# A two-block network on one core: the attention block takes tokens before their norm factor, and the factor is applied to the projections

## The chip, the cores and the metric

One core of a Trainium2 chip runs the whole program. The metric is the device time of one execution in microseconds; lower is better. In the profile the engines are PE (matrix multiply; PEld its weight loads), DVE (vector), ACT (scalar), POOL (GpSimd) and SP (which issues the DMAs). Each runs its own instructions strictly in program order and waits on semaphores for the others.

## The reference, cut to what matters

256 tokens of width 1024, float32. The first block has two layers: a mixer and a dense feed-forward, then a mixer and a mixture of eight experts (two a token); it ends in an RMS norm. The second block is an attention block over 16 learned meta tokens and the 256 tokens:

```python
x = first_block(...)                       # ends: rms_norm(x, norm_final)
h = concatenate([pad, meta, x])
xn = rms_norm_2(h, norm_gain)
proj = xn @ w_in                           # sb_q sb_k sb_v sw_q sw_k sw_v sb_z sw_z g_sb g_sw
o_sb = stick_breaking_attention(sb_q, sb_k, sb_v)       # 8 heads of 64
o_sw = sliding_window_sink_attention(rope(sw_q), rope(sw_k), sw_v, sinks)   # 16 heads on 2
y_sb, y_sw = (o_sb * silu(sb_z)) @ w_sb, (o_sw * silu(sw_z)) @ w_sw
h = h + (sigmoid(g_sb) * y_sb + sigmoid(g_sw) * y_sw) @ w_out
out = rms_norm_2(h, final_norm_gain)
```

So a token is normed twice in a row on its way into `w_in`: x·r1·gf (end of block one), then ·r2·g2. Per token both norms are one number r = r1·r2 and one row of weights gf·g2, and r can be applied before the projection or to its results.

## The kernel before, in words

Every matrix product is made of three float32r products: each operand is split into a high part (`whi`, `hi`) and the rest (`wlo`, `lo`), and PE adds hi·hi, hi·lo and lo·hi (`mm3`, L341 to L343). A weight unit is 128x1024 values. `Stream` (L158) brings raw tiles of two units by DMA, and `split` turns each unit into `whi` on ACT (L226) and `wlo` on DVE or POOL (L228), as the `plan` says per tile. `next` hands units to PE and splits some units ahead; every engine does its part at that place of its own order.

Experts: 88 chunks of 256 hidden columns. Chunk c does the two halves of its gate and up products, transposes chunk c-1's activation (`aH` on ACT, `aL` on DVE) and multiplies it by the down weights (`y`). `overflow` at chunk 85 is a branch round a large body that runs only when an expert has more than 128 tokens. After the last chunk `combine` adds the eighth expert's result to the tokens.

Entry to attention (`c_norms`, `phase_c`): per half of the tokens, sum of squares of x, x·gf, sum of squares of that, both factors, x·gf·r2·g2, PE transposes to `hT` (hi copied by ACT, lo subtracted by DVE), with 20 idle products (`warm`) on PE. Then the values `pv`, the keys and queries of the stick-breaking heads (8 projections `pj`), and a loop over those heads.

That loop is threaded with 38 further projections of 128 columns, the fills F0 to F37, in the order k, v, q0, z0, q1, z1, ... q7, z7, z8 to z11, g0 to g15. A fill is 24 matmuls into one of two PSUM buffers (tag `mm`), so fill n+2 waits until fill n's result has been read. `F` issues a fill and then the second steps of earlier ones: for q (and k) ACT copies the result (L1713), POOL turns it by the rope in six instructions (L1719 to L1721), and one fill later DVE and POOL place it as `qs` (L1469, L1470). For z and g ACT copies the result at once (L1476).

Iteration i of the loop (i = 0 to 7): `sb2(i)` (PE `sp`, DVE `lb` L1690, ACT exponent), F for q_i, `sb1(i+2)` (PE `zs`; three logs on ACT, `s`, `lb`, `sL` on DVE), F for z_i, and at odd i `sb3` (PE `av`). Then eight turns j of the sliding attention with two fills each: `sw1b(j)` scales the probabilities `pr` on DVE (L1783 to L1790), `sw1(j+1)` makes scores `sc` and their softmax (DVE reductions L1762, L1763, ACT exponents L1776), `sw2(j)` transposes (`pT`, L1800), `sw2b(j)` multiplies by the values (`ov`, L1818). `sw1(0)` runs in iteration 7 after that iteration's first fill.

Of the kernel before, what the change touches and what calls it, by code (L numbers as in the profile page):

```python
# [36 lines left out]
C_ID, C_BD, C_TRI, C_IOTA, C_LT, C_G2 = 0, 128, 256, 384, 512, 576  # L37
# [120 lines left out]
class Stream:  # L158
# [99 lines left out]
class K:  # L258
# [92 lines left out]
    def plan(self):  # L351
# [23 lines left out]
        if self.stop != "B":  # L375
            p += [(I["w_c"][i], i < 2 or 16 <= i < 24) for i in range(35)]
        return p

    def run(self):
        nc, tc = self.nc, self.tc  # L380
        with ExitStack() as es:
# [5 lines left out]
            ring = en(tc.tile_pool(name="ring", bufs=1))  # L387
            self.x = self.cs.tile([P, 2, D], F32, tag="x", name="x")
            self.con = self.cs.tile([P, C_N], F32, tag="con", name="con")
# [18 lines left out]
            if self.stop != "CX":  # L408
                with tc.tile_pool(name="ringx", bufs=1) as ringx, ExitStack() as es2:
                    self.W.add(ringx, self.RAW[1], self.HL[1])  # L410
                    self.ph = es2.enter_context(tc.tile_pool(name="ph", bufs=1))
# [9 lines left out]
            else:  # L421
                self.c_loads()
                self.c_g2()
                self.c_meta()
                self.c_meta2()
                self.c_rows()
                with tc.tile_pool(name="pj", bufs=1) as pj:
                    self.c_norms([lambda ns: 0] * 2, pj.tile([P, 512], F32, tag="junk", name="junk"))
# [8 lines left out]
    def phase_a(self):  # L437
# [4 lines left out]
        nc.sync.dma_start(self.con[:, P:], I["consts"][:, P:])  # L442
# [338 lines left out]
    def gln1b(self, g):  # L781
        self.nc.tensor.matmul(g[0][:, S:], self.con[:, C_BD:C_BD + P], g[1], start=True, stop=True)
# [141 lines left out]
    def phase_b(self):  # L924
# [8 lines left out]
        for c in range(N + 1):  # L933
# [18 lines left out]
            if 0 < c <= N:  # L952
# [3 lines left out]
                w = self.W.next(2, ahead=4 if c < N - 1 else 2)  # L956
# [7 lines left out]
            if c < N and e % 2 == 1 and e + 1 < NE:  # L964
# [4 lines left out]
                elif i == 9:  # L969
                    self.onehot_t(e // 2 + 1)  # L970
            if c == N - 3:
# [12 lines left out]
        if self.stop != "B":  # L984
            self.c_norms(comb, self.t2("junk"))
# [187 lines left out]
    def overflow(self):  # L1173

        nc, tc, pb = self.nc, self.tc, self.pb
        n = nc.values_load(self.cnt[0:1, 0:1], min_val=0, max_val=S)
# [5 lines left out]
        w = self.ph.tile([P, 2048], F32, tag="hx2", name="ov_w")  # L1182
# [4 lines left out]
        with tc.If(n > P):  # L1187
# [75 lines left out]
    def c_meta2(self):  # L1263
# [4 lines left out]
        self.metaT = self.cs.tile([P, KD, NM], F32, tag="metaT", name="metaT")  # L1268
        nc.scalar.activation(self.metaT, p[:, 0:P].rearrange("p (k t) -> p k t", k=KD), AF.Copy)
# [6 lines left out]
    def c_norms(self, before, junk):  # L1276

        nc, sm = self.nc, self.sm
        V, A = nc.vector, nc.scalar
        xn = [sm.tile([P, D], F32, tag="xn", name="xn", bufs=2) for _ in range(2)]  # L1280
        ss, v, r = [[sm.tile([P, n], F32, tag=t, name=t, bufs=2) for _ in range(2)]
                    for t, n in (("ss4", 4), ("nv", 3), ("nr", 2))]
        half = [slice(h * 512, h * 512 + 512) for h in range(2)]
        self.cx = [(xn[b], r[b]) for b in range(2)]

        def add(b, n):
            before[b](ns=(n,))
            x = self.x[:, b, half[n]]
            A.activation(junk, x, AF.Square, scale=1.0 / 32, accum_out=ss[b][:, n:n + 1])

        def gain(b, n, eng=V):
            y = xn[b][:, half[n]]
            eng.tensor_mul(y, self.x[:, b, half[n]], self.gf[:, half[n]])

        def power(b, n):
            y = xn[b][:, half[n]]
            A.activation(junk, y, AF.Square, scale=1.0 / 32, accum_out=ss[b][:, 2 + n:3 + n])

        def root(b):
            s, t = ss[b], v[b]  # L1300
            V.tensor_scalar(t[:, 0:1], s[:, 0:1], s[:, 1:2], EPS, op0=ALU.add, op1=ALU.add)
            V.scalar_tensor_tensor(t[:, 2:3], t[:, 0:1], EPS, s[:, 2:3], op0=ALU.mult, op1=ALU.add)
            V.tensor_add(t[:, 1:2], t[:, 2:3], s[:, 3:4])
            nc.gpsimd.tensor_tensor(r[b], t[:, 0:2], self.mhalf[:, 0:1].to_broadcast([P, 2]), op=ALU.pow)

        def scale(b, n):
            y = xn[b][:, half[n]]
            V.scalar_tensor_tensor(y, y, r[b][:, 1:2], self.g2[:, half[n]], op0=ALU.mult, op1=ALU.mult)
        for n in range(2):
            add(0, n)  # L1310
            gain(0, n)
            power(0, n)
        add(1, 0)
        root(0)
        self.W.release()
        self.W.ahead(3)
        add(1, 1)
        self.warm(20)
        scale(0, 0)
        gain(1, 0)  # L1320
        scale(0, 1)

        def rest():
            gain(1, 1)
            power(1, 0)
            power(1, 1)
            root(1)
            scale(1, 0)
            scale(1, 1)
        self.c_rest = rest  # L1330

    def phase_c(self):
        nc, pc, W, I = self.nc, self.pc, self.W, self.I
        V, A, mm = nc.vector, nc.scalar, nc.tensor.matmul
        hT = [pc.tile([P, KD, NK], F32R, tag="hT%d" % i, name="hT") for i in range(2)]
        self.split_small(self.metaT, *[t[:, :, 0:NM] for t in hT])
        W.ahead(4)
        self.transpose_split(self.cx[0][0], hT[0], hT[1], NM)
        self.c_rest()
# [3 lines left out]
        self.rep16 = self.t1("rep16")[0:48, 0:P]  # L1343
        for r in (slice(0, 32), slice(32, 48)):
            nc.vector.tensor_copy(self.rep16[r].rearrange("p (h c) -> p h c", h=8),
                                  self.ident[r, r.stop - NM:r.stop].unsqueeze(1).to_broadcast([r.stop - r.start, 8, NM]))
# [17 lines left out]
        def v_part(t, i):  # L1364
            for k in (2 * i, 2 * i + 1):
                if t < 2:
                    self.mm3(pv[t], [h[:, k, t * P:t * P + P] for h in hT], ws[k], k == 0, k == 7)
                else:
                    for j in range(2):
                        mm(pv[2][0:48, :], hl[:, k, :], ws[k][j], start=(k + j == 0), stop=(k + j == 8))  # L1370
        for i in range(4):
            ws += W.next(2, 1, 3 - i, True)
            v_part(0, i)
            if i == 1:
                self.transpose_split(self.cx[1][0], hT[0], hT[1], NM + P)
# [5 lines left out]
        A.activation(v01[:, 0, :], pv[0], AF.Copy)  # L1381
# [5 lines left out]
        V.tensor_copy(v01[:, 1, :], pv[1])  # L1387
        vl = self.t2("vl")
        V.tensor_copy(vl[0:48, :], pv[2][0:48, :])
        for b in range(2):  # L1390
            x = self.x[:, b, :]
            nc.gpsimd.tensor_scalar(x, x, self.cx[b][1][:, 0:1], None, op0=ALU.mult)
            nc.gpsimd.tensor_mul(x, x, self.gf)
# [17 lines left out]
        for j in range(4):  # L1411
            p = proj1(hT, NK)
            a, b = 2 * j, 2 * j + 1
            A.activation(kz[0:64, a, :], p[0:64, 0:S], AF.Copy)
            V.tensor_copy(kz[64:P, b, :], p[64:P, 0:S])
            V.tensor_copy(kp[0:64, j, a * NM:(a + 1) * NM], p[0:64, S:NK])
            V.tensor_copy(kp[64:P, j, b * NM:(b + 1) * NM], p[64:P, S:NK])
        q = pc.tile([P, 4, S], F32, tag="o4", name="q", bufs=4)
        for j in range(4):
            p = proj1(hx, S)  # L1420
            A.activation(q[:, j, :], p[:, :S], AF.Copy, scale=0.125)
# [31 lines left out]
        def f_v(j):  # L1453
            p = proj1(hT, NK)
            A.activation(vsT, p[:, :NK], AF.Copy)
# [18 lines left out]
        def f_c(dst):  # L1474
            p = proj1(hx, S)
            A.activation(dst, p[:, :S], AF.Copy)  # L1476
        def f_g(j):
            f_c(gs[0][:, j, :] if j < 8 else gs[j // 4 - 1][:, j % 4, :])
# [7 lines left out]
        def F():  # L1486
            late.append(next(fill)())
            later = [f() for f in late[:-1] if f]
            late[:-1] = [f for f in later if callable(f)]
# [65 lines left out]
        F()  # L1555
# [302 lines left out]
```

## Time and profile before

| | us |
|---|---|
| median of 3 runs | 1491.05 (1489.65 to 1492.88) |
| the profiled execution, its own time | 1494.97 |
| its span, first to last instruction | 1493.2 |
| PE busy in it | 1454.2 (97%) |
| DVE busy | 1162.2 (78%) |
| ACT busy | 957.7 (64%) |
| POOL busy | 285.5 (19%) |

The mean granted clock of TensorE is 0.989 of its full 2.4 GHz. The busy shares are means over stages with different limits: up to about 1200 us the experts run, the last 290 us are the attention block, where POOL does most of its work.

### The profile page before, as it was taken

How to read it: one execution, taken by the hardware profiler on the slowest of the kernel's cores; microseconds unless marked ns; L12 is line 12 of the kernel's file. 1: busy time of each engine (PE TensorE's matmuls, PEld its weight loads, DVE VectorE, ACT ScalarE, POOL GpSimd, SP SyncE). 2: the span in 40 equal slices, each digit the busy share in tenths (PEclk: the TensorE clock that was granted, in tenths of full speed). 3: DMA queues.
4: the chain of work that ended last, by engine and by line, in shares of the span. 5: the costliest groups of instructions: out<-in, count | busy, mean ns of one | idle time of the engine just before them, and what ended most of it. 6: DMA issues, size and time to landing. Idle time of an engine off the chain costs nothing. (4 is left out here: it accounts for less than half of the span.)

```text
span 1493.2 us, 21588 instructions
## 1 busy us (share of the span) xinstructions
PE 1454.2 (97%) x8166; PEld 1246.3 (83%) x8166; DVE 1162.2 (78%) x1571; ACT 957.7 (64%) x1412; POOL 285.5 (19%) x192
## 2 busy tenths in 40 slices
PE   9999999999999999999999999999999989988997
PEld 7979999989878888888888888877888769988996
DVE  5975544579689998999989999888999865656565
ACT  5654434465577777777777777776777654555653
POOL 4760000066300000000000000000000062885511
PEclk9999999999999999999999999999999999999999
DMA  9525555444579899999999998987999523333343
GB/s 359 190 86 211 181 207 191 150 157 188 197 297 373 305 351 340 347 369 368 352 331 353 361 370 300 351 308 291 373 357 363 212 108 142 114 113 114 142 177 119
DMA packets 59911, 381.43 MB, mean 255 GB/s; under 512 B 6787, under 2 KB 7171, under 8 KB 19094
## 3 DMA queue, kind: packets, MB, share of 16 engines
q1 hardware_dynamic: 59798, 379.96, 68.8%
q8 instruction: 66, 1.08, 0.3%
q14 instruction: 47, 0.39, 0.1%
HBM read 378.89 MB, written 1.05 MB: 254 GB/s over the span
## 5 line engine op out<-in xcount | busy, mean ns | idle before, releaser
L228 DVE TENSOR_TENSOR wlo<-raw,whi 128x1024 fp32r<-128x1024 f32 x647 | 767.9, 1233 | 113.3 <-ACT whi L226 104.3
L226 ACT ACTIVATE whi<-raw 128x1024 fp32r<-128x1024 f32 x712 | 710.5, 1052 | 47.9 <-issue 17.3
L341 PE MATMUL gu<-whi,hx 128*128 128x512 f32 x704 | 285.5, 406 | 2.1 <-PEq L1187 2.1
L343 PE MATMUL gu<-whi,hx 128*128 128x512 f32 x704 | 278.2, 395 | 0.0
L342 PE MATMUL gu<-wlo,hx 128*128 128x512 f32 x704 | 276.4, 393 | 0.0
L228 POOL TENSOR_TENSOR wlo<-raw,whi 128x1024 fp32r<-128x1024 f32 x65 | 159.3, 2478 | 391.3 <-ACT whi L226 387.2
L343 PEld LDWEIGHTS gu<-whi,hx 128*128 128x128 f32 x704 | 132.9, 189 | 30.5 <-DVE hx L1125 0.3
L341 PEld LDWEIGHTS gu<-whi,hx 128*128 128x128 f32 x704 | 133.0, 189 | 29.3 <-issue 3.3
L342 PEld LDWEIGHTS gu<-wlo,hx 128*128 128x128 f32 x704 | 133.3, 189 | 26.1
L280 POOL TENSOR_TENSOR rs_r<-rs_v,mh 128x1 f32<-128x1 f32 (+2 forms) x21 | 18.8, 900 | 674.7 <-DVE rs_v L279 674.7
L341 PE MATMUL mm<-h,whi 128*128 128x256 f32 x512 | 146.0, 285 | 0.0
L343 PE MATMUL mm<-h,wlo 128*128 128x256 f32 x512 | 145.0, 283 | 0.6 <-POOL wlo L228 0.6
L342 PE MATMUL mm<-h,whi 128*128 128x256 f32 x512 | 144.8, 283 | 0.0
L343 PE MATMUL y<-whi,aL 128*128 128x512 f32 x352 | 139.3, 396 | 1.6 <-DVE aL L336 1.6
L341 PE MATMUL y<-whi,aH 128*128 128x512 f32 x352 | 139.3, 396 | 0.0
L342 PE MATMUL y<-wlo,aH 128*128 128x512 f32 x352 | 139.2, 396 | 0.0
L335 ACT ACTIVATE aH<-tr 128x256 fp32r<-128x256 f32 x90 | 34.4, 384 | 116.4 <-PE tr L1144 116.2
L343 PE MATMUL pj<-hT,wlo 128*128 128x256 f32 (+1 forms) x368 | 104.3, 283 | 3.0 <-DVE wlo L228 2.9
L341 PE MATMUL pj<-hT,whi 128*128 128x256 f32 (+1 forms) x368 | 107.1, 291 | 0.0
L342 PE MATMUL pj<-hT,whi 128*128 128x256 f32 (+1 forms) x368 | 103.7, 282 | 0.0
L342 PEld LDWEIGHTS mm<-h,whi 128*128 128x128 f32 x512 | 98.1, 192 | 1.1 <-issue 0.5
L341 PEld LDWEIGHTS mm<-h,whi 128*128 128x128 f32 x512 | 98.1, 192 | 1.1 <-DVE pc L767 0.2
(362 smaller groups left out, 2347.3 us busy)
## 6 DMA issues: line engine op xcount, KB each, us to landing
raw<-w_moe SPq DMA_DIRECT2D x227, 1024.0 KB, 6.6
raw<-w_moe SPq DMA_DIRECT2D x74, 512.0 KB, 6.5
raw<-w_c SPq DMA_DIRECT2D x35, 1024.0 KB, 4.8
raw<-w_mix SPq DMA_DIRECT2D x23, 1024.0 KB, 5.1
raw<-w_gu SPq DMA_DIRECT2D x22, 1024.0 KB, 4.8
raw<-w_d SPq DMA_DIRECT2D x11, 1024.0 KB, 4.7
row<-rows SPq DMA_DIRECT2D x3, 512.0 KB, 5.7
x<-x SPq DMA_DIRECT2D x2, 512.0 KB, 3.9
```

What stands on the lines that cost most here:

```text
L226: nc.scalar.activation(hl[0], src, AF.Copy)
L228: (nc.gpsimd if pool is True or pool and pool[h] else nc.vector).tensor_sub(hl[1], src, hl[0].bitcast(F32))
L280: nc.gpsimd.tensor_tensor(r, v, self.mhalf[:, 0:1].to_broadcast([P, n]), op=ALU.pow)
L335: nc.scalar.activation(hi, src, AF.Copy)
L341: mm(out, a, c, start=start, stop=False)
L342: mm(out, a, d, start=False, stop=False)
L343: mm(out, b, c, start=False, stop=stop)
```

## The change

The count of the largest expert is loaded into registers at chunk 2 instead of in `overflow`, and a hint for the branch is placed at chunk 84. The last expert tile is put into buffers that end with the experts, so that the attention block's first four weight units can be split during the last two chunks. `c_norms` becomes `c_enter`: it multiplies the tokens by gf·g2 only, transposes and splits them; the squares, the two factors and a row R with r of every token are made later by `c_factor`, and each projection is multiplied by R (or, for values, by a column `rv`) where it leaves PSUM, on DVE. The 20 idle products go. The residual x·r1·gf moves from POOL to DVE (`resid`). The z and g results, copied by ACT at once before, are now multiplied on DVE in a second step, one fill later. Of the w_c tiles 0 to 5 and 16 to 23, whose `wlo` came from POOL (0, 1, 16 to 23) or DVE, now the first unit is DVE's and the second POOL's (both DVE's for tile 0). `sw1(0)` moves ahead of iteration 7's first fill. A 128x128 constant gets a DMA and a buffer of its own.

```diff
 class Stream:
+    def early(self, r, free):
+        if r == self.cut - 1:
+            for i, t in enumerate(free):
+                if id(t) not in self.late:
+                    del free[i]
+                    return t
     def fetch(self, n=1000):
-            t = self.slot(self.raw_free, self.nf >= self.cut)
+            t = self.early(self.nf, self.raw_free)
+            if self.nf != self.cut - 1:
+                t = self.slot(self.raw_free, self.nf >= self.cut)
     def split(self, u):
-            hl = self.slot(self.hl_free, r >= self.cut)
+            hl = self.early(r, self.hl_free) or self.slot(self.hl_free, r >= self.cut)
...
-            p += [(I["w_c"][i], i < 2 or 16 <= i < 24) for i in range(35)]
+            p += [(I["w_c"][i], (False, 0 < i < 6 or 16 <= i < 24)) for i in range(35)]
...
-                w = self.W.next(2, ahead=4 if c < N - 1 else 2)
+                w = self.W.next(2, ahead=4)
...
+            if c == 2:
+                self.most = nc.values_load(self.cnt[0:1, 0:1], min_val=0, max_val=S)
+            if c == N - 4:
+                self.tc.mark_branch_hint_location("most", engines=[...])
...
-            self.c_norms(comb, self.t2("junk"))
+            self.c_enter(comb)
...
     def c_meta2(self):
-        nc.scalar.activation(self.metaT, ..., AF.Copy)
+        self.split_small(p, h[:, :, 0:NM], h[:, :, NM:2 * NM])
+        nc.vector.tensor_mul(self.g2, self.g2, self.gf)
...
+    def c_enter(self, before):
+        u = [sm.tile([P, D], F32, tag="xn", name="xn", bufs=2) for _ in range(2)]
+        def add(b, n):
+            before[b](ns=(n,))
+            V.tensor_mul(u[b][:, half[n]], self.x[:, b, half[n]], self.g2[:, half[n]])
+        def turn(b, q):
+            p = self.pt("tr")
+            for k in range(4):
+                c = (q * 4 + k) * P
+                nc.tensor.transpose(p[:, k * P:(k + 1) * P], u[b][:, c:c + P], self.ident)
+            A.activation(self.hT[0][dst], pv, AF.Copy)
+            return lambda: V.tensor_sub(self.hT[1][dst], pv, self.hT[0][dst].bitcast(F32))
+        self.W.release()
+        add(0, 0)
+        add(0, 1)
+        turn(0, 0)()
+        add(1, 0)
+        turn(0, 1)()
+        add(1, 1)
+        self.c_turn = turn
+    def c_factor(self):
+        for b in range(2):
+            for n in range(2):
+                V.tensor_mul(y, self.x[:, b, c], self.gf[:, c])
+                A.activation(junk, self.x[:, b, c], AF.Square, ...)
+                A.activation(junk, y, AF.Square, ...)
+        # three small DVE operations, pow on POOL, then
+        V.tensor_tensor(d, self.ident..., r[:, 1, :]..., op=ALU.mult)
+        mm(p[:, 0:S], self.ones, d.rearrange("p b t -> p (b t)"), start=True, stop=True)
+        A.activation(R[:, NM:], p[:, 0:S], AF.Copy)
+        # four products of one column turn R into rv; two DVE copies
+        V.tensor_mul(cs, cs, R.unsqueeze(1).to_broadcast([P, 2, NK]))
...
     def phase_c(self):
-        self.transpose_split(self.cx[0][0], hT[0], hT[1], NM)
-        self.c_rest()
...
+        v_part(0, range(4))
+        lo = [self.c_turn(1, 0), self.c_turn(1, 1)]
+        v_part(0, range(4, 8))
+        for f in lo:
+            f()
...
+        v_part(1, range(4))
+        v_part(1, range(4, 8))
+        self.c_factor()
         for i in range(4):
-            for t in (1, 2):
-                v_part(t, i)
+            for k in (2 * i, 2 * i + 1):
+                for j in range(2):
+                    mm(pv[2][0:48, :], hl[:, k, :], ws[k][j], ...)
             W.release(1)
             W.ahead(2)
...
-            nc.gpsimd.tensor_scalar(x, x, self.cx[b][1][:, 0:1], None, op0=ALU.mult)
-            nc.gpsimd.tensor_mul(x, x, self.gf)
+        def resid(b):
+            for h in range(2):
+                V.scalar_tensor_tensor(x, x, self.r1[:, b:b + 1], self.gf[:, c], op0=ALU.mult, op1=ALU.mult)
...
         def f_c(dst):
             p = proj1(hx, S)
-            A.activation(dst, p[:, :S], AF.Copy)
+            def rest():
+                V.tensor_mul(dst, p[:, :S], R[:, NM:])
+            return rest
...
         for i in range(8):
             self.sb2(i)
+            if i == 7:
+                self.sw1(0, qs, ks)
             F()
             if i == 3:
                 self.sw_setup(vsT)
+            if i in (2, 4):
+                resid(i // 2 - 1)
             if i < 6:
                 self.sb1(i + 2, kz, q)
-            if i == 7:
-                self.sw1(0, qs, ks)
             F()
```

## Rows read from the trace of the kernel before

**Rows 1.** Waits of PE over the span: total us, times, longest

```profile
PE pT L1800 <- DVE pr L1789: 5.3, 1, 5.3
...
PE gu L341 <- PEq L1187: 2.1, 1, 2.1
```

**Rows 2.** Instructions of line L1187, the branch: duration ns, start us

```profile
L1187 PEldq COMPARE_BRANCH x1: 5267/5267/5267, 1175.3 to 1175.3; - x1
```

**Rows 3.** Timeline, end of the experts: start, us, instruction, idle before, releaser

```profile
1196.62 2.36 DVE L228 TENSOR_TENSOR wlo<-raw,whi 128x1024 fp32r<-128x1024 f32 x2 [0.53 <-ACT whi L226]
...
1199.37 0.50 PE L343 MATMUL y<-whi,aL 128*128 128x512 f32 x1 [0.66 <-DVE aL L336]
...
1201.57 0.39 PE L343 MATMUL y<-whi,aL 128*128 128x512 f32 x1
```

**Rows 4.** Timeline, entry to the attention block

```profile
1206.26 0.69 DVE L1293 TENSOR_TENSOR xn<-x,row 128x512 f32<-128x512 f32 x1
1206.41 0.63 ACT L1289 ACTIVATE junk<-x 128x512 f32<-128x512 f32 x1
1206.87 0.75 DVE L1171 SCALAR_TENSOR_TENSOR x<-cb,gate,x 128x512 f32<-128x512 f32 x1
...
1214.03 0.47 PE L341 MATMUL pv<-whi,hT 128*128 128x512 f32 x1
...
1233.92 0.29 PE L341 MATMUL pj<-hT,whi 128*128 128x272 f32 x1
```

**Rows 5.** Stretch of the entry: length, busy us by engine, granted clock, DMA

```profile
1214.03:1221.80 7.77, 6.36 (x20) 4.85 (x21) 6.17 (x11) 1.99 (x6) 4.23 (x4) 0.56 0.61 243
```

**Rows 6.** Timeline of PE, from the start of fill F5 (z1) to that of F7 (z2)

```profile
1279.25 0.37 PE L341 MATMUL pj<-hT,whi 128*128 128x256 f32 x1
...
1283.29 0.65 PE L1703 MATMUL av<-lb,v 128*64 128x256 f32 x2
...
1284.67 0.45 PE L1686 MATMUL sp<-sH,triR 128*128 128x400 f32 x1
...
1285.50 0.36 PE L341 MATMUL pj<-hT,whi 128*128 128x256 f32 x1
...
1288.43 0.35 PE L1669 MATMUL zs<-nR,iR 128*128 128x400 f32 x1
...
1289.19 0.37 PE L341 MATMUL pj<-hT,whi 128*128 128x256 f32 x1
```

**Rows 7.** Timelines of DVE and POOL in the stick-breaking loop

```profile
1282.48 1.23 DVE L228 TENSOR_TENSOR wlo<-raw,whi 128x1024 fp32r<-128x1024 f32 x1 [1.55 <-ACT whi L226]
1285.14 0.61 DVE L1469 CAST qs<-rq 64x256 fp32r<-64x256 f32 x2 [1.44 <-POOL rq L1721]
...
1293.98 0.61 DVE L1469 CAST qs<-rq 64x256 fp32r<-64x256 f32 x2 [1.44 <-POOL rq L1721]
...
1344.03 1.59 POOL L1721 TENSOR_TENSOR rq<-rq,rr 128x256 f32<-128x256 f32 x1
```

**Rows 8.** Stretches round PE's longest idle time; columns as in rows 5

```profile
1340.00:1348.20 8.20, 1.32 (x10) 0.93 (x8) 5.24 (x9) 4.55 (x14) 7.51 (x8) 0.76 0.26 80
1348.20:1352.00 3.80, 3.80 (x21) 3.60 (x22) 3.53 (x15) 0.77 (x4) 1.49 (x2) 0.61 0.25 103
```

**Rows 9.** Pieces of the chain that ended last, sliding attention: start, us

```profile
1353.29 0.59 PE ov L1818 x8
...
1361.65 0.59 PE ov L1818 x8
```

**Rows 10.** Timelines of DVE and POOL in the sliding attention

```profile
1365.91 0.31 DVE L1762 TENSOR_REDUCE swst<-sc 128x1 f32<-128x144 f32 x1 [2.64 <-PE sc L1761]
...
1371.40 4.81 POOL L228 TENSOR_TENSOR wlo<-raw,whi 128x1024 fp32r<-128x1024 f32 x2 [3.52 <-ACT whi L226]
...
1424.00 2.41 POOL L1552 TENSOR_TENSOR o<-o,z 128x1024 f32<-128x1024 f32 x1 [0.35 <-ACT o L1842]
...
1424.90 2.59 DVE L228 TENSOR_TENSOR wlo<-raw,whi 128x1024 fp32r<-128x1024 f32 x1 [5.10 <-ACT whi L226]
```

More of the change, by code (lines that the diff above doesn't have):

```diff
@@ L970, in phase_b @@
                     self.onehot_t(e // 2 + 1)
+            if c == 2:
+                self.most = nc.values_load(self.cnt[0:1, 0:1], min_val=0, max_val=S)
+            if c == N - 4:
+                self.tc.mark_branch_hint_location("most", engines=[getattr(mybir.EngineType, e) for e in ("PE", "DVE", "Activation", "Pool", "SP")])
             if c == N - 3:
@@ L1186, in overflow @@
         p, pg = self.pt("tr", "ov_p"), self.pt("mm", "ov_g")
-        with tc.If(n > P):
+        with tc.If(self.most > P, label="most"):
             for e in range(NE):
@@ L1271, in c_rows @@
+        nc.vector.tensor_mul(self.g2, self.g2, self.gf)
     def c_rows(self):
         self.gf = self.c_row(64)
-    def c_norms(self, before, junk):
+    def c_enter(self, before):
         nc, sm = self.nc, self.sm
         V, A = nc.vector, nc.scalar
-        xn = [sm.tile([P, D], F32, tag="xn", name="xn", bufs=2) for _ in range(2)]
-        ss, v, r = [[sm.tile([P, n], F32, tag=t, name=t, bufs=2) for _ in range(2)]
-                    for t, n in (("ss4", 4), ("nv", 3), ("nr", 2))]
+        u = [sm.tile([P, D], F32, tag="xn", name="xn", bufs=2) for _ in range(2)]
+        self.hT.append(self.ph.tile([P, KD, NK], F32R, tag="hx3", name="hT"))
+        V.tensor_copy(self.hT[1][:, :, 0:NM], self.hT[0][:, :, NM:2 * NM].bitcast(F32))
@@ L1299, in root @@
[L1299 to L1312, printed above, removed]
+            V.tensor_mul(u[b][:, half[n]], self.x[:, b, half[n]], self.g2[:, half[n]])
[4 more added lines that the diff above has]
+                nc.tensor.transpose(p[:, k * P:(k + 1) * P], u[b][:, c:c + P], self.ident)
+            pv = p.rearrange("p (k t) -> p k t", k=4)
+            dst = (slice(None), slice(q * 4, q * 4 + 4), slice(NM + b * P, NM + (b + 1) * P))
+            A.activation(self.hT[0][dst], pv, AF.Copy)
+            return lambda: V.tensor_sub(self.hT[1][dst], pv, self.hT[0][dst].bitcast(F32))
@@ new lines, in c_factor @@
+    def c_factor(self):
+        nc, sm, pc = self.nc, self.sm, self.pc
+        V, A, mm = nc.vector, nc.scalar, nc.tensor.matmul
+        ss = sm.tile([P, 4, 2], F32, tag="ss4", name="ss4", bufs=2)
+        v = sm.tile([P, 2, 2], F32, tag="nv", name="nv", bufs=2)
+        r = sm.tile([P, 2, 2], F32, tag="nr", name="nr", bufs=2)
+        self.r1 = r[:, 0, :]
+        t = pc.tile([P, 4 * S], F32, tag="z4", name="junk", bufs=3)
+        junk = t[:, 512:]
+        for b in range(2):
+            for n in range(2):
+                c = slice(n * 512, n * 512 + 512)
+                y = t[:, 0:512]
+                V.tensor_mul(y, self.x[:, b, c], self.gf[:, c])
+                A.activation(junk, self.x[:, b, c], AF.Square, scale=1.0 / 32, accum_out=ss[:, n, b:b + 1])
+                A.activation(junk, y, AF.Square, scale=1.0 / 32, accum_out=ss[:, 2 + n, b:b + 1])
+        V.scalar_tensor_tensor(v[:, 0, :], ss[:, 0, :], EPS, ss[:, 1, :], op0=ALU.add, op1=ALU.add)
+        V.scalar_tensor_tensor(v[:, 1, :], v[:, 0, :], EPS, ss[:, 2, :], op0=ALU.mult, op1=ALU.add)
+        V.tensor_add(v[:, 1, :], v[:, 1, :], ss[:, 3, :])
+        nc.gpsimd.tensor_tensor(r.rearrange("p a b -> p (a b)"), v.rearrange("p a b -> p (a b)"),
+                                self.mhalf[:, 0:1].to_broadcast([P, 4]), op=ALU.pow)
+        d = self.t1("rd").rearrange("p (b t) -> p b t", b=2)
+        V.tensor_tensor(d, self.ident.unsqueeze(1).to_broadcast([P, 2, P]),
+                        r[:, 1, :].unsqueeze(2).to_broadcast([P, 2, P]), op=ALU.mult)
+        p = self.pt("tr", "rp")
+        mm(p[:, 0:S], self.ones, d.rearrange("p b t -> p (b t)"), start=True, stop=True)
+        R = self.R
+        A.activation(R[:, NM:], p[:, 0:S], AF.Copy)
+        one = self.ones[0:1, 0:1]
+        p = self.pt("tr", "rv")
+        for t in range(2):
+            mm(p[:, t:t + 1], R[0:1, t * P:(t + 1) * P], one, start=True, stop=True)
+        mm(p[0:32, 2:3], R[0:1, NK - 32:], one, start=True, stop=True)
+        mm(p[32:48, 2:3], R[0:1, NK - NM:], one, start=True, stop=True)
+        self.rv = pc.tile([P, 3], F32, tag="rv", name="rv")
+        V.tensor_copy(self.rv[:, 0:2], p[:, 0:2])
+        V.tensor_copy(self.rv[0:48, 2:3], p[0:48, 2:3])
+        cs = self.cc[:, D_COS:D_COS + 2 * NK].rearrange("p (a t) -> p a t", a=2)
+        V.tensor_mul(cs, cs, R.unsqueeze(1).to_broadcast([P, 2, NK]))
@@ L1334, in phase_c @@
         V, A, mm = nc.vector, nc.scalar, nc.tensor.matmul
-        hT = [pc.tile([P, KD, NK], F32R, tag="hT%d" % i, name="hT") for i in range(2)]
-        self.split_small(self.metaT, *[t[:, :, 0:NM] for t in hT])
-        W.ahead(4)
-        self.transpose_split(self.cx[0][0], hT[0], hT[1], NM)
-        self.c_rest()
+        hT = self.hT
+        R = self.R = pc.tile([P, NK], F32, tag="R", name="R")
+        V.memset(R[:, 0:NM], 1.0)
         hl = self.t2("hl", F32R)[:, :KD * 48].rearrange("p (k t) -> p k t", k=KD)
[L1343 to L1346, printed above, removed]
         kz = pc.tile([P, 8, S], F32, tag="m8", name="kz", bufs=3)
@@ L1484, in phase_c, with F @@
         late = []
-        def F():
+        def F(last=False):
             late.append(next(fill)())
-            later = [f() for f in late[:-1] if f]
-            late[:-1] = [f for f in later if callable(f)]
+            n = len(late) - (not last)
+            later = [f() for f in late[:n] if f]
+            late[:n] = [f for f in later if callable(f)]
         self.sb_setup1(kp, q, v01, vl)
```

98 lines of the change are left out of this document (39 added, 59 removed).

## Prediction

> **What bounds the kernel now.** I read the waits of PE first. PE is almost always busy, so what the change can give lies in the few places where it isn't, and what it can cost lies in new waits of PE. Three places matter. At the branch round the overflow body PE stands for 2.1 us, and its branch instruction alone lasts 5.27 us [rows 1, 2]. At the entry to attention the last expert product starts at 1201.57, the first value product only at 1214.03 and the first key projection at 1233.92 [rows 3, 4]; from 1214.03 to 1221.80 the granted clock is a mean 0.56, the lower of the two levels for most of that time [rows 5]. In the sliding attention PE waits 5.3 us for DVE's `pr` [rows 1], and after that hole the clock is a mean 0.61 from 1348.2 to 1352.0 [rows 8].
>
> Next I read DVE and POOL in the stick-breaking loop. DVE copies a turned query (`qs`) at 1285.14 and the next at 1293.98, 8.84 us apart, and each time it has stood 1.44 us for POOL's last rope instruction [rows 7]: POOL sets this pace. PE runs ahead of it: F5 (z1) starts at 1279.25 [rows 6], 5.9 us before DVE copies q0. In the sliding attention PE sets the pace: one turn is 1361.65 - 1353.29 = 8.36 us [rows 9], and DVE stands 2.64 us in it for PE's scores [rows 10].
>
> **Branch and last experts.** The early count takes the register loads from the branch and the hint may take the fetch. The gain is between 0 and the 2.1 us that PE stands; I take 1.6, since both parts of the wait are attacked and neither is priced by a row. Against it: chunk 87 now splits four units where it split two, ahead of the last `aH` and `aL`. Two `wlo` take DVE 2.36 us, and PE already waits 0.66 us for `aL` behind such a pair [rows 3], so two more cost 2.4 us, or nothing if they find no free buffer; I take 2.4. They have their raw tile in time, as SP no longer holds the first attention tiles back for a buffer that the last expert tile has; that tile's own DMA goes two splits later, still a chunk and more ahead of its use, and a late one would show as ACT waiting for it.
>
> **Entry.** Now from the last `y` product's end, 1201.96, to the key projection it is 32.0 us [rows 3, 4]. After: DVE's order is four combines (0.75), four multiplies (0.69) and two subtractions of about the multiply's size [rows 4]. PE transposes the first quarter after two of them, and three more instructions lie between it and the second quarter, so value products start about 5.4 us after `y` ends. Products of 512 columns come every 0.24 us (ten from 1199.37 to 1201.57 [rows 3]): 48 of them, with eight short transposes (1 us, an estimate), are 12.4 us. Meanwhile ACT runs the eight squares, 0.63 us each [rows 4], with accumulator reads some 6 us, beside the last 36 products (8.6 us). With two copies ahead of the squares and the root chain behind them, the factor comes about when PE ends or up to 3 us later; I take 1 us late, plus 1.5 us in which PE makes R and `rv` with ACT's copy between. The last 16 products, 3.8 us, follow. Sum 24.1, a gain of 7.9 us. Bounds: 10.4 if the factor costs PE nothing, 5 if the clock falls here again (half speed for some 6 of the 7.8 us [rows 5]).
>
> **Stick-breaking loop.** This is where I expect the loss. z0's result was copied by ACT at once; now DVE multiplies it in the step after q0's `place`, and DVE meets that `place` first and stands there for POOL. So z0's PSUM buffer comes free after 1285.14 + 0.61 [rows 7] + 0.45, the multiply, an estimate from 0.69 for twice its columns [rows 4]. F5 needs this buffer and started at 1279.25 [rows 6]. It will start near 1286.3, 7 us later; POOL's own start may slip by 0.5 more, as `vsT` is on DVE too. The multiply reads PSUM; it can't pass the `qs` ahead of it.
>
> From there PE is tied into the ring. After z's buffer is free: fill 2.93 (1285.50 to 1288.43), at odd iterations `av` 1.38, `sp` 0.83 [rows 6]; then DVE's `lb` (some 0.6), 1.55 in which ACT makes the exponent and the next `whi`, `wlo` 1.23, `qs` 0.61 [rows 7], the multiply 0.45, and some 0.4 of signals: 8.6 at even iterations, 10.0 at odd. POOL's 8.84 holds the even ones, so the mean is 9.4 against 8.84, over five steps 2.8 us. `resid` adds four DVE instructions of 0.75, half hidden: I count 1 us. In iteration 7 the early scores put the softmax (about 3.5 us on DVE and ACT) ahead of `wlo` and `qs` of q6, so z7 starts 3.5 us later again. Sum for the start of z7: 7.5 + 2.8 + 1 + 3.5, some 15 us later than now, relative to F4. Part comes back: before, PE was busy for 1.32 of the 8.2 us from 1340, so 6.9 idle, and lost 0.39 of the next 3.8 us, 1.5, to the clock [rows 8]. Sum: +6.4 us at the end of F19, bounds +3 and +10. One hole of 6 to 7 us before F5 is longer than the 5.3 us after which the clock fell [rows 8]; half speed for some 3.7 us costs 1.9 us (0 to 4).
>
> **Sliding attention.** At each turn's first fill the `wlo` goes from POOL to DVE and, with the multiply of the fill before, lands ahead of `sw1b`. It needs a `whi` that ACT makes after the exponents, two copies and another `whi`: 0.4 + 2 x 1.0 + 1.2 + 0.45, about 4 us between softmax and `sw1b`, where 2.64 us are spare [rows 10]: +1.3 us a turn, or +0.8 with DVE's own waits for POOL taken out. Here a second cost comes on top: POOL's `wlo` takes 2.4 us (4.81 for two) and starts one `whi` earlier than DVE's; a DVE `wlo` that met a POOL instruction running from 1424.00 to 1426.41 took 2.59 us instead of 1.23 [rows 7, 10]: 1.5 us more. I take 2.3 a turn: five turns and a first wait of 1.2 make +12.7 us; bounds 4 and 14.
>
> The Trainium skill says of this (SBUF — State Buffer, section "Who interferes with whom") that a VectorE instruction with two SBUF inputs and a GpSimd instruction that reads SBUF exclude each other for the whole instruction. By that rule DVE and POOL gain nothing from taking a `wlo` each at the same time, and the turn lasts 10.6 us; without it, 9.2. The row of 2.59 us agrees with it.
>
> **At nothing.** The extra DMA of a constant on SP's queue lies under the first transfers (0 to 0.4). The product g2·gf in chunk 70 is one DVE instruction of `wlo`'s size, 1.2 us, under four units split ahead (0 to 1.2). Key and query results are now read by DVE alone, at most four short reads of 0.45 under a projection of 2.93 us [rows 6].
>
> **Sum.** -1.6 + 2.4 - 7.9 + 6.4 + 1.9 + 12.7 = +13.9 us. The profiled execution took 1494.97, so 1508.9 by its own time; it lies 3.9 above the median of the runs, which gives 1505. The likeliest case's own range is 1496 to 1512.
>
> **Rivals.**
> - *Faster.* The early scores do what they are for: `sw1(0)` leaves the queue behind q6's copy, and the hole at `pr` goes, 8.4 us with its clock, while ACT, free of 28 copies, keeps the rings short. Then only the entry and the branch count: -7.1 - 8.4 = -15.5, 1475.5, or about 1484 with the hole half filled. For it: ACT is in both rings. Against it: it decides at F5, where DVE would have to reach z0's multiply by 1279.25 and not at 1285.75. Chance 0.25.
> - *Given back.* Only the stick-breaking loop pays, and in the sliding attention DVE gets its `wlo` in before POOL: turns at 8.4 to 9.2 us. +1.2 to +5.5, 1492 to 1496.5. Chance 0.22, nearly half of it within 0.2% (some 3 us, about what a measurement of this kernel tells from no change).
> - *The hint does nothing.* PE stands as before at the branch; 1.6 us more in any case, no case of its own.
>
> My forecast has 0.53. So faster 0.25, same 0.10, slower 0.65. The range 1483 to 1512 leaves out the full gain below and both loops at their upper bounds above.
>
> **What would show it.** Right: PE waits at F5 for DVE's multiply of z, 5 us or more; `qs` to `qs` over 9 us; turns of the sliding attention over 9 us with PE waiting for `pr` in each; a DVE `wlo` of some 2.5 us beside POOL's; key projections 24 us after the last `y`; no wait over 1 us at the branch. Wrong: z multiplied before POOL ends the rope; turns still 8.4 us; the low clock at the entry.

## The result, and the profile after

The change makes the kernel slower: 1502.08 us median of 4 runs (1501.51 to 1505.2) against 1491.35 of the kernel before in runs beside it, ratio 1.0065, 95% interval 1.0049 to 1.0082. The forecast was 1505, slower, so direction, size and range held. Its sum held less well: two terms are wrong by more than 4 us each, on opposite sides, so part of the agreement is luck.

The profiled execution took 1502.27 us by its own time, span 1500.6. The waits of PE in it (total, times, longest; against [rows 1]):

```profile
PE pj L351 <- ACT rq L1765: 9.2, 5, 3.2
PE pT L1852 <- DVE pr L1841: 7.5, 6, 1.3
PE pj L351 <- DVE gw L1523: 4.0, 3, 1.6
...
PE pj L351 <- DVE kp L1462: 0.9, 1, 0.9
```

The wait at the branch and the one of 5.3 us for `pr` are gone. In their place PE waits in many small pieces: five times for ACT's copy of a query (`rq`), six times for `pr`, three times for a `gw` multiply. To see what each stage cost, take the same PE instructions in both traces. Rows of before that were not shown yet (the product behind the branch, the first and seventh `ov`):

```profile
1180.72 0.47 PE L341 MATMUL gu<-whi,hx 128*128 128x512 f32 x1 [2.12 <-PEq L1187]
...
1353.21 0.45 PE L1818 MATMUL ov<-pt,vs 128*64 128x128 f32 x4
...
1403.24 0.56 PE L1818 MATMUL ov<-pt,vs 128*64 128x128 f32 x6
```

and the same of after, from the timeline of PE (start, length; the last bracket is the idle time before and what ended it):

```profile
1176.04 0.47 PE L351 MATMUL gu<-whi,hx 128*128 128x512 f32 x1
...
1195.10 0.50 PE L351 MATMUL y<-whi,aH 128*128 128x512 f32 x1 [1.51 <-ACT aH L345]
...
1196.99 0.50 PE L353 MATMUL y<-whi,aL 128*128 128x512 f32 x1 [1.16 <-DVE aL L346]
...
1199.19 0.39 PE L353 MATMUL y<-whi,aL 128*128 128x512 f32 x1
...
1204.93 0.40 PE L1400 MATMUL pv<-whi,hT 128*128 128x512 f32 x1
...
1223.75 0.29 PE L351 MATMUL pj<-hT,whi 128*128 128x272 f32 x1
...
1344.77 0.67 PE L1870 MATMUL ov<-pt,vs 128*64 128x128 f32 x8
...
1406.04 0.43 PE L1870 MATMUL ov<-pt,vs 128*64 128x128 f32 x3
```

| PE starts | before | after | difference | step | forecast |
|---|---|---|---|---|---|
| product behind the branch | 1180.72 | 1176.04 | -4.68 | -2.1 at the branch, -2.6 ahead of it | -1.6, 0 |
| last `y` product | 1201.57 [rows 3] | 1199.19 | -2.38 | +2.3, chunk 87 | +2.4 |
| first key projection | 1233.92 [rows 4] | 1223.75 | -10.17 | -7.8, entry | -7.9 |
| first `ov` | 1353.21 | 1344.77 | -8.44 | +1.7, stick-breaking loop | +8.3 |
| seventh `ov` | 1403.24 | 1406.04 | +2.80 | +11.2, six turns | +12.7 |
| end of the span | 1493.2 | 1500.6 | +7.4 | +4.6, tail | 0 |

The 2.6 us ahead of the branch can't be put down to the change: there the two kernels do the same products, and the runs below on the changed kernel, which have its instructions up to there, reach this product between 1174.79 and 1178.34 in their profiles. The profile of before was a long one: it stands 3.6 us above the median of 1491.35, that of after 0.2 above its own, which is why the medians differ by 10.7 and the profiles by 7.3.

### The profile page after: what moved, and what is told of

It is laid out like the page before. It is cut to its first block, busy times and chain, and to the rows that moved or that the text cites. A ratio compares the mean times of both kernels' runs of the same rounds, so it can differ in the third digit from the quotient of the medians.

```text
span 1500.6 us, 21551 instructions
## 1 busy us (share of the span) xinstructions
PE 1449.8 (97%) x8136; PEld 1238.3 (83%) x8136; DVE 1185.6 (79%) x1623; ACT 946.6 (63%) x1375; POOL 255.9 (17%) x180
## 5 line engine op out<-in xcount | busy, mean ns | idle before, releaser
L238 DVE TENSOR_TENSOR wlo<-raw,whi 128x1024 fp32r<-128x1024 f32 x654 | 784.4, 1245 | 122.3 <-ACT whi L236 114.4
L238 POOL TENSOR_TENSOR wlo<-raw,whi 128x1024 fp32r<-128x1024 f32 x58 | 142.5, 2489 | 431.7 <-ACT whi L236 424.4
L352 PEld LDWEIGHTS mm<-h,whi 128*128 128x128 f32 x512 | 96.4, 188 | 1.5 <-issue 0.5
L351 PEld LDWEIGHTS mm<-h,whi 128*128 128x128 f32 x512 | 96.5, 188 | 1.1 <-issue 0.2
```

The costliest lines, as they stand in the source:

```text
L351: mm(out, a, c, start=start, stop=False)
L352: mm(out, a, d, start=False, stop=False)
```

## The experiments

Each kernel below is the changed kernel with the edit shown, unless it says "before". Times are medians; ratios are to the kernel before, in runs beside them. Its median was 1491.35 beside the change and 1492.58 to 1493.93 beside the runs below, so a difference of two medians from different sets is good to some 2 us.

**The turn of the sliding attention: who makes `wlo`.** Four runs change who makes `wlo` for w_c tiles 16 to 23, and nothing else. The last leaves POOL's half out of the program.

```diff
-  (I["w_c"][i], (False, 0 < i < 6 or 16 <= i < 24))
+  (I["w_c"][i], 16 <= i < 24 or (False, 0 < i < 6))   # p_pool: both units on POOL
+  (I["w_c"][i], (16 <= i < 24, 0 < i < 6))            # p_swap: POOL first, DVE second
+  (I["w_c"][i], (False, 0 < i < 6))                   # p_dve: both on DVE
...
+  if not (h and 16 <= c < 24):                        # no_pool_wlo: POOL's unit left out
       (nc.gpsimd if ... else nc.vector).tensor_sub(hl[1], src, hl[0].bitcast(F32))
```

> The changed kernel with one edit undone: for w_c tiles 16 to 23 both wlo go back to POOL. Theory (the DVE wlo ahead of sw1b, locked against POOL's, makes the turn of the sliding attention): the turn falls from 10.20 to PE's own 8.4 us, six turns, the waits of PE for pr (six, 7.5 us) go, and the kernel takes 9 to 11 us less, about 1492. Rival (the multiply of z and g on DVE ahead of pr makes the turn, wherever wlo is made): turns stay at 9.2 us or more and no more than 6 us come back.

> The changed kernel with the two engines of w_c tiles 16 to 23 exchanged: POOL makes the first unit's wlo of each tile, DVE the second's, so in a turn DVE's wlo follows the earlier of the two whi. Theory (order and lock together): DVE's wlo takes 1.23 us again, or meets POOL's only at its end, and is done 2.2 us earlier (1.05 for the earlier whi, 1.3 for the lock); the ring through DVE and ACT falls from 10.2 to about 8 us, PE's 8.4 sets the turn, and 8 to 11 us come back, as with POOL alone. Rival (it is the load on DVE): a turn of 9 us or more, less than 7 us back.

> The changed kernel with both wlo of w_c tiles 16 to 23 on DVE and none on POOL. Theory (the lock is 1.3 us of the turn): with no POOL instruction beside it the wlo takes 1.23 us, two of them end 1.1 to 1.3 us earlier than the one of 2.58 does now, and the turn is about 9.1 us against 10.20, so DVE is faster with twice the work there: 5 to 7 us back. Rival (a wlo of 2.58 us is DVE's own doing, or DVE's load counts): turns of 10.2 us or more, nothing back.

> The changed kernel without POOL's wlo in the sliding attention: for w_c tiles 16 to 23 the second unit's rest is not computed, and its buffer keeps an older one; all else as in the changed kernel. Theory (the lock, and nothing else, stretches DVE's wlo and with it the turn): wlo takes 1.23 us, the ring through DVE and ACT falls by 1.35 from 10.20 to 8.85 us. Rival (the order alone, as the runs with DVE's wlo first in the turn or with two on DVE might say): the turn stays at 10.2 us.

Measured: p_pool 1492.92 (ratio 1.0006, 0.9991 to 1.0020), 9.2 less than the change, and the turn is 8.42 (PE's `pT` in p_pool):

```profile
1367.96 0.82 PE L1852 MATMUL pT<-con,pr 128*128 128x128 f32 x6
...
1376.38 0.82 PE L1852 MATMUL pT<-con,pr 128*128 128x128 f32 x6
```

p_swap 1508.56 (1.0117, 1.0090 to 1.0144) and p_dve 1511.99 (1.0114, 1.0087 to 1.0142): both slower than the change, where 5 to 11 us less was expected. no_pool_wlo, one execution: 1495.46.

First the change itself, DVE and POOL in one turn, then PE behind them:

```profile
1367.65 2.58 DVE L238 TENSOR_TENSOR wlo<-raw,whi 128x1024 fp32r<-128x1024 f32 x1 [3.14 <-ACT whi L236]
1370.15 0.41 DVE L1523 TENSOR_TENSOR gs<-pj,R 128x256 f32<-128x256 f32 x1
...
1371.02 0.28 DVE L1841 TENSOR_SCALAR pr<-pr,swst 128x128 f32<-128x128 f32 x1
...
1366.75 2.40 POOL L238 TENSOR_TENSOR wlo<-raw,whi 128x1024 fp32r<-128x1024 f32 x1 [7.80 <-ACT whi L236]
...
1371.45 1.21 PE L1852 MATMUL pT<-con,pr 128*128 128x128 f32 x6 [1.23 <-DVE pr L1841]
```

DVE's `wlo` starts 0.9 us behind POOL's, lasts 2.58 us instead of 1.23 and ends 1.1 us after POOL's: this standing of one engine beside an instruction of the other is called the lock below. Then come the multiply and `pr`, for which PE waits. A turn is 10.20 us (1371.45 against 1361.25 for the `pT` before). Without POOL's `wlo` (no_pool_wlo, timelines of DVE and PE):

```profile
1367.09 1.23 DVE L240 TENSOR_TENSOR wlo<-raw,whi 128x1024 fp32r<-128x1024 f32 x1 [3.14 <-ACT whi L236]
...
1360.68 1.21 PE L1854 MATMUL pT<-con,pr 128*128 128x128 f32 x6
...
1369.53 1.21 PE L1854 MATMUL pT<-con,pr 128*128 128x128 f32 x6
```

`wlo` is 1.35 us shorter and so is the turn: 8.85 (one of six is 9.34). So of the 1.85 us that a turn grew, 1.35 is the lock; the 0.5 left is what DVE's `wlo` of 1.23 us and the multiply cost in that place. But p_dve shows that the lock is not needed for a long turn:

```profile
1374.03 1.23 DVE L238 TENSOR_TENSOR wlo<-raw,whi 128x1024 fp32r<-128x1024 f32 x1 [2.52 <-ACT whi L236]
1375.17 0.42 DVE L1523 TENSOR_TENSOR gs<-pj,R 128x256 f32<-128x256 f32 x1
...
1375.74 0.36 PE L351 MATMUL pj<-hT,whi 128*128 128x256 f32 x1 [1.94 <-DVE gs L1523]
```

Here, and in p_swap, a DVE `wlo` stands ahead of the multiply of an earlier fill. It waits 2.52 us for ACT's `whi`, which comes after the exponents; the multiply behind it holds a PSUM buffer, and PE waits 1.94 us for that in each turn, which is 10.4 us in both. My theory named one ring, `wlo` to `pr`; a second one through the multiply is as long, and an earlier `wlo` only trades one for the other. This second ring is read from PE's waits; no run takes the multiply out of it. In each of these places a DVE `wlo` made the turn longer than the 8.42 us that p_pool has.

**The stick-breaking loop.** Why was the hole at F5 3.2 us and not 7? The timelines of PE, ACT and DVE of the changed kernel there:

```profile
1273.67 0.38 PE L351 MATMUL pj<-hT,whi 128*128 128x256 f32 x1 [3.19 <-ACT rq L1765]
...
1273.25 0.36 ACT L1765 ACTIVATE rq<-pj 128x256 f32<-128x256 f32 x1
...
1276.67 0.42 DVE L1523 TENSOR_TENSOR z<-pj,R 128x256 f32<-128x256 f32 x1
```

and the stretches of the hole and of F5 (columns as in [rows 5]; the granted clock is the third number from the right):

```profile
1270.48:1273.67 3.19, 0.01 (x2) 0.00 (x1) 1.64 (x3) 1.81 (x4) 3.00 (x4) 1.00 0.32 98
1273.67:1278.23 4.56, 4.56 (x25) 4.43 (x25) 3.03 (x7) 2.12 (x5) 3.93 (x5) 0.63 0.39 163
```

F5 starts 3 us before z0 is multiplied. It can't have z0's buffer; it has that of F4 (q1), the fill just before it, and it starts when ACT has copied q1. In the program ACT's copy of q1 stands ahead of z0's multiply, so q1's buffer comes free first and is given out first. The edit that tests it multiplies z at the head of the next fill's step:

```diff
 def F(last=False):
+    while first:
+        first.pop(0)()          # z and g multiplies
     late.append(next(fill)())
...
 def f_c(dst):
...
-    return rest
+    first.append(rest)
```

> The changed kernel, but the multiply of a z or g result stands at the head of the next fill's step, ahead of that fill's splits and of its ACT copy, and not behind them. Theory (F5 and its like wait because they are given the PSUM buffer of the fill just before, which ACT copies late, while z's buffer comes free later in program order): the fills z1 to z7 wait for the z result before and start sooner; of the 9.2 us that PE waits for ACT's rq copies in five places 3 to 6 go, and the low clock behind the longest with them; 3 to 7 us less. Rival (POOL's rope or DVE's ring sets the pace of the stick-breaking loop): PE waits as long in another place, 0 to 1 us less.

Measured: 1495.78 (ratio 1.0023, 1.0009 to 1.0036), 6.3 less than the change, inside the theory's range. All five waits for `rq` (9.2 us) are gone, and three of 5.4 us for z multiplies stand in their place; F5 now waits for z0, 1.83 us in place of 3.19. By the profiles 2.3 us come back in the stick-breaking loop, the stage that the theory was about, 0.6 in the six turns, 4.6 in the tail and 1.2 ahead of the branch: what F5 is given is shown, but the size was met with the help of a stage that the expectation did not name. Its row, and the stretches of its hole and of F5:

```profile
1271.20 0.36 PE L351 MATMUL pj<-hT,whi 128*128 128x256 f32 x1 [1.83 <-DVE z L1523]
```

```profile
1269.37:1271.20 1.83, 0.00 (x1) 0.03 (x1) 1.69 (x3) 0.45 (x2) 1.77 (x2) 1.00 0.02 4
1271.20:1275.76 4.56, 4.56 (x25) 4.34 (x26) 1.99 (x4) 2.87 (x6) 3.95 (x5) 0.63 0.64 230
```

The low clock behind it stayed, which the expectation had wrong. The early scores were tested by moving them back:

```diff
-    if i == 7:
-        self.sw1(0, qs, ks)
     F()
...
+    if i == 7:
+        self.sw1(0, qs, ks)
     F()
```

> The changed kernel with the first scores of the sliding attention back in their old place, behind iteration 7's first fill and sb1. Theory (the early scores fill the hole before the first pT, 6.9 us of idle time and 1.5 us of low clock in the kernel before, and pay some 3 us for it at the last z fill): PE waits for pr before the first pT again, 4 to 7 us, the last z fill starts 1.5 to 3 us sooner, and the kernel takes 3 to 6 us more, 1505 to 1508. Rival (the prediction's: the early scores cost 3.5 us at z7, and the hole is filled by DVE's lateness anyway): 1 to 3 us less.

Measured: 1503.31 (ratio 1.0061, 1.0041 to 1.0080). The median is 1.2 more than the change's and the ratio a little less, so these runs can't tell it from no difference, and both sets of numbers missed. The hole at the first `pT` comes back at 1.60 us, with 1.76 for a z multiply behind it; in return the wait of 1.99 us at the last z fill and the low clock behind it go, but the clock is 0.64 from 1340.5 to 1348.9, behind the hole that came back. The early scores move a hole and the low clock with it, and are worth about nothing.

**The branch.** The kernel before, with the early count alone (b_load) and with the hint (b_hint):

```diff
+    if c == 2:
+        self.most = nc.values_load(self.cnt[0:1, 0:1], min_val=0, max_val=S)
+    if c == N - 4:                                     # b_hint alone
+        self.tc.mark_branch_hint_location("most", engines=[...])
...
-        with tc.If(n > P):
+        with tc.If(self.most > P, label="most"):
```

> The kernel before with one part of the change alone: the count is loaded into registers at chunk 2, and the branch has a name, but no hint is placed. Theory A (the register loads at the branch are the stall): PE no longer stands 2.12 us there, about 1.5 to 2 us less. Theory B (the jump over the large body and the fetch of what follows are the stall, and the hint removes it): the branch still lasts about 5 us on PE and PE stands 1.5 to 2.1 us, 0 to 0.5 us less.

> The kernel before with the early count and the hint at chunk 84, and nothing else of the change. Both theories: no wait of PE over 0.3 us at the branch, 2.1 us less than before, 0.14%. If by the side of the run with the early count alone nothing changes, the hint does nothing.

Measured: b_load 1492.95 (ratio 0.9994, 0.9984 to 1.0005), b_hint 1489.71 (0.9974, 0.9964 to 0.9984). The branch on PE's queue in b_load, b_hint and after (duration ns), against 5267 in [rows 2]:

```profile
L1188 PEldq COMPARE_BRANCH  x1: 6262/6262/6262, 1172.4 to 1172.4; - x1
```

```profile
L1190 PEldq COMPARE_BRANCH  x1: 397/397/397, 1168.8 to 1168.8; - x1
```

```profile
L1203 PEldq COMPARE_BRANCH  x1: 397/397/397, 1171.6 to 1171.6; - x1
```

and PE's wait at it in b_load, with no such line in the other two:

```profile
PE gu L341 <- PEq L1188: 2.1, 1, 2.1
```

With the count loaded 83 chunks earlier PE still waits 2.1 us; with the hint it doesn't wait. The register loads cost PE nothing, and the hint is the whole gain: the rival "the hint does nothing" falls. The kernel before with these lines alone is 0.26% faster. Only 2.1 us of this show as a wait, while the interval is 2.4 to 5.4 us; in the profiles the rest lies ahead of the branch, and its cause stays open.

**Putting the good parts together.** combo1: `wlo` on POOL, multiplies first, and two units ahead at chunk 87. combo2: four units ahead again, multiplies first only for F0 to F17 and from F33 on. combo3: combo2 with the two copies of `rep16` moved ahead of the squares. combo4: combo3 with `sw1b` ahead of the first fill in every turn.

```diff
-    w = self.W.next(2, ahead=4)
+    w = self.W.next(2, ahead=4 if c < N - 1 else 2)    # combo1 alone
...
+    if 18 <= count[0] < 33:                            # combo2 to combo4
+        return rest
     first.append(rest)
...
-    if j in (0, 7):                                    # combo4
-        self.sw1b(j)
-        F()
-    else:
-        F()
-        self.sw1b(j)
+    self.sw1b(j)
+    F()
```

> The changed kernel with three edits: wlo of w_c tiles 16 to 23 on POOL, the z and g multiplies at the head of the next fill's step, and two units split ahead at chunk 87 where the change splits four. If the three add up: 9 us of the turns, 4 to 6 us of the stick-breaking loop and the tail, and 2.3 us of chunk 87 (PE's waits for aH and aL, 2.7 us, fall to 0.7), 1484 to 1488, faster than both kernels. Rival (the edits lie on one another: with POOL making wlo, POOL's rope or PE's own work sets the same pace; two units too few at the entry cost what chunk 87 gives back): 1489 to 1493.

> The changed kernel with two edits: wlo of w_c tiles 16 to 23 on POOL, and the multiplies at the head of the next fill's step for F0 to F17 and from F33 on; from F18 to F32, in the sliding attention, they stay behind it, as the change has them. Four units are split ahead at chunk 87, as in the change. Theory (in the run with all three edits, the multiply put pr two POOL instructions late in the sliding attention, and the entry lacked two units): turns of 8.42 us as with POOL alone, 3 us less in the stick-breaking loop, 2 us less in the tail: 1486 to 1489, faster than before. Rival (nothing adds up, since PE runs into DVE's pr sooner when it comes earlier): 1490 to 1494.

> As combo2, with the two small copies of rep16 moved from behind the value products to ahead of the squares, where POOL does not run a wlo. Theory (lock: two copies of 32x128 values take 3.24 us now beside two POOL instructions, and the first key results wait for them): the copies take about 0.3 us, the wait of PE for kp (0.93 us) goes, 1 us less than combo2. Rival (the wait moves to the next wlo): no difference from combo2.

> As combo3, with sw1b ahead of the turn's first fill in every turn of the sliding attention (the change has it there in the first and the last alone): pr no longer stands behind the multiply of the fill before. Theory (two modes: a turn of 8.42 us where pr starts ahead of POOL's first wlo, 9.67 us where it starts behind it and meets both; 0.1 us decides, and the multiply's wait for PE puts pr late): all pr are done when POOL starts, no pr over 0.4 us, every turn 8.42 us, and the time is that of combo3 or 1 us less, 1485 to 1488. Rival (the multiply comes later now and holds the PSUM buffer): PE waits for DVE's z or gs, 1 us a turn, 1492 to 1495.

Measured: combo1 1495.57 (ratio 1.0004, 0.9990 to 1.0018), combo2 1496.55 (1.0009, 0.9990 to 1.0028), combo3 1487.12 (0.9957, 0.9940 to 0.9973), combo4 1487.03 (0.9963, 0.9950 to 0.9977). The first two missed; the last two are faster than both kernels. combo3 was to take 1 us less than combo2 and took 9.4 less, for another reason than the one expected (below).

combo1 shows that the two extra units of chunk 87 give back what they cost: without them the profile is 2.3 us shorter there (20.89 against 23.15 us from the product behind the branch to the last `y`; PE no longer waits for `aH`, and 0.66 for `aL`) and 2.2 us longer from there to the first key projection (26.72 against 24.56), where PE then waits 1.03 for `yL` and 1.70 for a `wlo`. So that +2.3 of the change is the price of its entry.

combo1 and combo2 have turns of 9.67 us, though their plan is p_pool's, with 8.42. DVE, POOL and PE in a turn of combo2:

```profile
1378.14 2.45 DVE L1849 TENSOR_SCALAR pr<-pr,swst 128x128 f32<-128x128 f32 x1
...
1380.52 2.46 DVE L1850 TENSOR_SCALAR pr<-pr,swst 128x256 f32<-128x256 f32 x1
...
1378.07 4.76 POOL L238 TENSOR_TENSOR wlo<-raw,whi 128x1024 fp32r<-128x1024 f32 x2 [4.93 <-ACT whi L236]
...
1383.03 0.44 PE L1860 MATMUL pT<-con,pr 128*128 128x128 f32 x2 [1.05 <-DVE pr L1850]
```

Two scalings of 0.3 us each take 2.45 us: each stands beside one POOL instruction. In combo3, whose instructions in the turn are the same, the scaling of 128x128 is ahead of POOL, and only the last one stands at POOL's start (2.52 us in one turn, 0.34 in the next):

```profile
1372.72 0.28 DVE L1849 TENSOR_SCALAR pr<-pr,swst 128x128 f32<-128x128 f32 x1
...
1372.90 4.95 POOL L238 TENSOR_TENSOR wlo<-raw,whi 128x1024 fp32r<-128x1024 f32 x2 [3.52 <-ACT whi L236]
```

The same loop thus ran at 8.42 and at 9.67 us a turn. A quarter of a microsecond in its phase seems to decide (POOL starts 0.07 us ahead of that scaling in combo2, 0.18 behind it in combo3); of combo3's gain over combo2, 7.7 us in the profiles are these turns. Why two copies at the entry moved the phase stays open. combo2's twelve times fall in two groups, 2 at 1486.8 to 1487.5 and 10 at 1493.3 to 1499.2; that these are the two turns is likely (1.25 x 6 = 7.5 us) but only one execution was profiled. combo4 was to take `pr` off this edge and did not: its last scaling starts 0.02 us behind POOL, as in combo3 (1372.92 and 1372.90).

```profile
1374.58 0.35 DVE L1846 TENSOR_SCALAR pr<-pr,swst 128x256 f32<-128x256 f32 x1
...
1374.56 4.96 POOL L238 TENSOR_TENSOR wlo<-raw,whi 128x1024 fp32r<-128x1024 f32 x2 [3.52 <-ACT whi L236]
```

Most of its turns are 8.48 with `pr` short, but the last scaling of the eighth turn takes 2.50 us and PE waits 0.96 for it, where no `pr` over 0.4 was expected. Its times, 1485.4 to 1490.9, are those of combo3 (1485.8 to 1490.2).

combo3 also shows the lock at the entry. In the changed kernel two copies of 32x128 values stood beside POOL and held up the first key results, which is PE's wait of 0.9 us for `kp`. DVE and POOL of after:

```profile
1223.18 3.24 DVE L1426 COPY rep<-con 32x128 f32<-32x128 f32 x2
...
1223.03 2.50 POOL L238 TENSOR_TENSOR wlo<-raw,whi 128x1024 fp32r<-128x1024 f32 x1 [5.44 <-ACT whi L236]
1225.48 0.87 POOL L1450 CAST nR<-neg 128x816 fp32r<-128x816 f32 x1
```

Moved to where POOL is idle, the two take 0.51 us and PE no longer waits for `kp`; PE's wait for `rd` grew from 1.1 to 1.6.

## Why the prediction was right, and where not

- *Branch, -1.6: measured -2.1.* Right; all of it is the hint's.
- *Chunk 87, +2.4: +2.3.* Right in size: 1.51 for `aH` and 1.16 for `aL` against 0.66 before. But it was priced as DVE's `wlo` ahead of `aL`, and the larger wait is for ACT, which makes four `whi` (3.89 us) ahead of `aH` where it made two (2.00). The lower bound, that the two units find no free buffer, is out.
- *Entry, -7.9: -7.8.* From the last `y` product's end, 1199.19 + 0.39, it is 24.17 us to the key projection; the forecast was 24.1. Value products started 5.35 us after it (5.4), 48 of them took 12.17 us (12.4), the factor 2.92 (2.5; PE waits 1.10 and 0.47 of it), and the last 16 products 3.73 (3.8). The clock didn't fall (the stretch from 1204.93 to 1223.75 was at 1.00). That is one execution: in the profile of p_dve, with the same instructions up to here, it was 0.81 from 1196 to 1202.9 and 0.92 in this stretch, and the step took 26.4 us.
- *"At nothing": +0.9.* The key results were late, by a lock and not by the reads that were priced.
- *Stick-breaking loop with its clock, +8.3: +1.7 with that 0.9.* This is the step that failed: "F5 needs this buffer and started at 1279.25. It will start near 1286.3, 7 us later". It does not need z0's buffer, as its start 3 us ahead of z0's multiply and z_first show, and the hole is 3.2. So the rule in the description of the kernel before, that fill n+2 waits until fill n's result has been read, does not hold here, where q1's result is read before z0's. The low clock behind it is as forecast (4.56 us for 2.93, +1.6 against +1.9). From the start of F4 to that of the last z fill, z7, it is 64.5 us (1266.53 to 1331.00) against 56.8 before (1275.56 to 1332.35): 7.7 us later with that clock, where 15 and 1.9 were forecast. Of the further 7.3 us in that 15 (ring 2.8, residual 1, early scores 3.5) no run singles out the first two; the scores turned out worth about nothing either way. What comes back behind z7 was near the forecast: 7.1 us up to the first `ov`, for 8.4.
- *Sliding attention, +12.7: +11.2.* The mechanism is right: a DVE `wlo` of 2.58 us, PE waiting for `pr` in each turn. The forecast had 10.6 us a turn by the lock, and 9.2 without; measured are 10.20 and, with POOL's `wlo` left out, 8.85. The Trainium skill (SBUF — State Buffer, section "Who interferes with whom") states such a lock, for two SBUF inputs on VectorE beside a GpSimd instruction that reads SBUF; the `wlo` of 2.58 us, which ends behind POOL's, agrees. Sizes were off twice: 1.85 us a turn and not 2.3 (lock 1.35 for 1.5, the rest 0.5 for 0.8), and six turns, not five and a first wait.
- *Tail, nothing: +4.6.* The prediction has no term for it. Multiplied one fill late, the last g results hold their buffers while DVE does the end of the sliding attention: three waits of 1.33, 1.07 and 1.65 us for `gw`. With the multiplies first (z_first) they are gone.

So +13.9 was forecast and +7.4 shown by the profiles, 10.0 without the 2.6 ahead of the branch: 6.6 too much in one loop and 1.5 in the other, 4.6 too little in the tail. The rival "given back" fell at the turns, 10.20 us and not 8.4 to 9.2. "Faster" fell since the hole at `pr` went but waits for `rq`, for `pr` in each turn and for `gw` took its place.

## What to carry to other kernels

When a result's last reader moves to another engine or a step later, look up which buffer the next producer is given: here it was the one freed first in program order, not the older one, and the wait may be on an instruction that the change never touched. Of two engines that share work beside a tight loop, ask not only how long each takes but what stands behind each piece on its queue; here a subtraction of 1.2 us, moved from POOL to DVE, stood ahead of what PE needed, and cost 9 us. A branch round a large body can be worth a hint (here 2.1 us of PE's waiting, and 0.26% of the kernel in time), which takes a few lines.

## What the hardware showed that was not expected

- Beside a POOL `wlo` even a tiny DVE instruction with both inputs in SBUF stands still: in p_swap the addition of 128x4 values takes 2.08 us, 0.14 in the changed kernel. The multiplies ahead of it, which read PSUM and one tile in SBUF, aren't stretched (0.75 for two, the second running when POOL starts). DVE and POOL of p_swap:

```profile
1379.15 0.75 DVE L1523 TENSOR_TENSOR gs<-pj,R 128x256 f32<-128x256 f32 x2
1379.82 2.08 DVE L1835 TENSOR_TENSOR swst<-swst 128x4 f32<-128x4 f32 x1
...
1379.48 2.38 POOL L238 TENSOR_TENSOR wlo<-raw,whi 128x1024 fp32r<-128x1024 f32 x1 [8.40 <-ACT whi L236]
```

- Scalings and copies with one tensor in SBUF are stopped as well (`pr` 2.45 for 0.28, `rep` 3.24 for 0.51, two copies). The same page and section of the Trainium skill names both kinds as able, under conditions, to take the pair of ports that VectorE shares with GpSimd; the rows agree.
- Idle time alone doesn't tell whether TensorE's clock falls behind a hole: after 1.83 us of it (z_first) and 1.99 the next 4.6 us ran at 0.62 to 0.63, after 1.95 at full clock. Windows of after, behind the holes of 1.99 and of 1.95 us:

```profile
1329.01:1331.00 1.99, 0.01 (x1) 0.01 (x1) 0.30 (x1) 1.99 (x7) 0.44 (x1) 1.00 0.00 0
1331.00:1335.55 4.55, 4.55 (x24) 4.40 (x25) 4.42 (x9) 0.89 (x1) 3.15 (x3) 0.62 0.12 14
...
1310.11:1312.06 1.95, 0.00 (x0) 0.00 (x1) 0.40 (x2) 1.81 (x4) 1.66 (x3) 1.00 0.73 143
1312.06:1315.10 3.04, 3.04 (x24) 2.91 (x24) 2.94 (x7) 2.11 (x5) 1.66 (x3) 1.00 0.60 253
```
